# Where the four weight sums of the out projection are made: beside the second half of a streaming-encoder layer's input projection, or beside its first half

## The chip, the cores and the metric

The kernel runs on one core of one Trainium2 chip. The metric is device time in microseconds (us) of one execution; lower is better. The kernel before was run three times for its time, and one further execution was recorded by the hardware profiler; all rows of the profile below are of that one execution. In the rows, PE is the matrix engine, PEld its loading of stationary operands, DVE the vector engine, ACT the scalar engine, POOL the general engine (GpSimd), SP the engine whose instruction queue issues nearly all DMAs here.

## The reference, cut to what matters

One layer on a sequence of 2048 tokens of width 1024, in f32:

```python
u = rms_norm(h, g_mix_pre)
z = u @ w_in                      # (2048,1024) @ (1024,2816)
ya = swa_with_sinks(q, k, v of z) # sliding-window attention, 512 of the columns out
yh = hgrn2(q, f, i, g of z)       # gated linear recurrence, 512 columns out
h = h + rms_norm(concat(ya, yh) @ w_out, g_mix_post)
h = h + rms_norm(cross_attention(...), g_x_post)
h = h + rms_norm((silu(u @ w_gate) * (u @ w_up)) @ w_down, g_ffn_post)
```

What matters here are two products, the input projection `u @ w_in` and the out projection `... @ w_out`, and what the kernel prepares for the second one while the first one runs.

## The kernel before

**Every f32 operand is split in two.** A value goes into a high part rounded to the matrix engine's format and a low part (the rest), and a product is three matmuls, high by high, high by low and low by high (`products`, L1123, lines 1131 to 1133). The high part is made by ACT or POOL, the low part by DVE (`split2`, L984: lines 987, 989, 990). A product of a 512-deep half is 12 matmuls of 128x128 by 128x512.

**Large products are done by seven half-size products instead of eight** (`seven`, L1135, in the order 1, 5, 6, 3, 7, 2, 4 of `STEPS`). The stationary side comes as seven tiles S, made two products ahead (`streamed`, L1065: sums of raw quarters by DVE at line 1106, splits at 987 to 990). The moving side needs, beside the four quarters of the operand, four sums and differences of quarters. For an operand that serves many blocks these four are formed once and kept in DRAM: `sums` (L1418) makes such a DRAM tile and a generator `combined` (L1027). For the out projection that tile is `out_s`. The weight's two halves of rows are treated in turn; of each half the generator makes the sums 5, 7, 6 and 4, and each of these eight rounds has the same form: issue the DMA loads of the quarters that are new into a first row tile and a second row tile, 128x1024 f32 each; pause three times; one DVE addition or subtraction of the two row tiles in place (line 1034); one DMA store of the result to `out_s`; pause once more. The sums 5, 7 and 6 are left in the first tile and stored from there, the sum 4 in the second:

```python
            for x, y, key in (((0, 1), (0, 0), 5), ((1, 1), (0, 1), 7), (None, (0, 0), 6), (None, (1, 0), 4)):
                if x:
                    t = get(0, *x, a, b - a)
                o = get(1, *y, a, b - a)
                for _ in range(3):
                    yield
                ...
                yield
```

Where rounds 6 and 4 have no `x`, the first tile is still that of round 7. `w_out` (L1411) loads a quarter of the weight in two DMAs for the upper rows and in one for the lower ones, which makes 20 loads in all. The addition is traced inside `behind` (L1050): it is queued after the last DVE instruction that was traced when `mark` (L1058) was last called.

**The stages.** The profile's span falls into these parts around the change:

- The input projection for the first 1024 tokens (`in_first`, L451), until about 238 us. Its work comes in blocks of two groups of 128 columns (`ORDER`, L419). Columns 4 and 5, and 0 and 1, are made in four plain blocks; then come nine blocks of seven products. Counted from zero these are blocks 4 to 12 of `phases` (L1219). Blocks 5 to 8 pair a group of the recurrence's forget gate (columns 10 to 13) with a group of its query (6 to 9); the `after` part of such a block (L659) runs beside the next block and makes the gate's decays (`decays`, L726): a logarithm on ACT, two running sums on DVE, exponentials on ACT.
- The same projection for the other 1024 tokens (`in_proj`, L684), interleaved with the sliding-window attention (`swa`) and the first half of the recurrence (`hgrn`), about 262 to 623 us.
- The second half of the recurrence beside the folding of the cross-attention's weights (`fold_cross`), then the out projection and the rest of the layer as a row of jobs of `phases`.

**What sets the order.** `phases` traces a block product by product. After each product it calls `mark`, traces the stationary tiles that are needed two products on, and then lets every generator in its list `after` run to its next pause. A job's last entry, `beside`, names generators that join this list when a block begins. `in_first` gives its job an empty one, `{}` (L536). From what is traced a planner builds each engine's queue: it lists the instructions by their place in the trace and by the moment at which its own cost table has them ready. On the chip each queue then runs in order; an instruction that waits holds up all that is behind it on its engine, and the SP queue does the same for DMAs.

**Where the sums are made before.** In `mix` (L194), after nine steps of the attention and after the first half of the recurrence, `mix` creates the generator (L228), takes its first step, and lets it make four steps (one sum) behind each of the attention's last eight steps (L236). The two row tiles come from the pool `io` of that stage, under the tags `u` (two buffers) and `x` (three buffers), `io_tile` L61.

**The tiles of the first stage.** Pool `st_pool` of the first stage has the tag `pair` (five buffers of 128x2048: outputs of a block, loaded tokens, decays), `part` and `sum`. The raw quarters of the weights (`sraw`) have three buffers. The DMAs of this stage, all in the SP queue, are the weight loads, loads of the later tokens of `x` (line 663), stores of normed tokens (`un_d`) and stores of the projection (`z_d`).

Of the kernel before, what the change touches and what calls it, by code (L numbers as in the profile page):

```python
# [11 lines left out]
F32 = mybir.dt.float32  # L12
# [6 lines left out]
P = 128  # L19
T = 2048  # L20
D = 1024
# [27 lines left out]
class Layer:  # L49
# [144 lines left out]
    def mix(self):  # L194
        tc, I = self.tc, self.I
        kw = dict(reuse_waits="tile")
        with contextlib.ExitStack() as left:
            def pool(name, at, **k):
                return at.enter_context(tc.tile_pool(name=name, bufs=1, **k, **kw))

            self.mc = pool("mc", left)
            self.r_x = self.cst.tile([P, NT], F32, name="r_x")
            with (
                tc.tile_pool(name="t1", bufs=3, **kw) as self.ts,
                tc.tile_pool(name="t2", bufs=3, **kw) as self.tb,
                tc.tile_pool(name="s1", bufs=2, side="right", **kw) as self.st_pool,
                contextlib.ExitStack() as at,
            ):
                self.banks(at, "ps1", **MOST)
                self.raws = 3  # L210
                u = self.in_first()
            self.banks(left, "ps2", **FOUR)
            self.hg = pool("hg", left)
            self.wp = pool("wp", left)
            self.io = pool("io", left)
            with tc.tile_pool(name="sw", bufs=1, side="right", **kw) as self.sw:
                self.zero_tiles()
                swa = self.swa(range(NT), lambda n: "st" if n < NPB else "sth")
                hgrn = self.hgrn(range(NPB), "h")
                cols = self.in_proj(1, u)  # L220
                next(cols)
                for _ in range(NPB + 1):
                    next(swa)
                    next(hgrn)
                    next(cols)
                for _ in hgrn:
                    pass
                self.out_sums, side = self.sums("out_s", self.w_out, 4, lambda: self.io_tile("u"), lambda: self.io_tile("x"))  # L228
                side = side()
                next(side)  # L230
                pairs = self.hgrn(range(NPB, NT), "gt")
                for i, _ in enumerate(swa, NPB + 2):
                    next(cols)
                    if i == NT + 1 - 0:
                        next(pairs)
                    for _ in range(4):  # L236
                        next(side, None)
                for _ in cols:
                    pass
            phases = self.phases(self.jobs(), None, lambda: self.io_tile("z"))  # L240
            with tc.tile_pool(name="xp", bufs=1, side="right", **kw) as self.xp:
                fold = self.fold_cross()
                for _ in range(2):
                    next(fold)
                for i, _ in enumerate(pairs, 1):
                    for _ in range(2):
                        next(fold)
                    if 2 <= i < 10:
                        next(phases)
                for _ in fold:  # L250
                    pass
            left.close()
            with (
                tc.tile_pool(name="t3", bufs=3, **kw) as self.ts,
                tc.tile_pool(name="t4", bufs=3, **kw) as self.tb,
                tc.tile_pool(name="s3", bufs=2, side="right", **kw) as self.st_pool,
                contextlib.ExitStack() as at,
            ):
                self.banks(at, "ps3", **MOST)
                self.raws = 4  # L260
                for _ in phases:
                    pass
# [188 lines left out]
    def in_first(self):  # L451
# [4 lines left out]
        def x_loads(s, tiles):  # L456
            if tiles[0] == 0:
                stage.append(self.tb.tile([P, 4, D], F32, tag="T", name=f"x0_{s}", bufs=3))
            for i in tiles:
                self.load(stage[s][:, i, :], I["x"][(4 * s + i) * P:(4 * s + i + 1) * P, :])  # L460
                if s + i == 0:
                    self.g_mix = self.gain(I["g_mix_pre"])

        x_loads(0, (0, 1))
        T, raw = {}, {}
# [51 lines left out]
        def fetch():  # L517
            for s in range(2):
                for q in range(2):
# [9 lines left out]
        blocks = [("s",) + self.in_block(*p, tokens[i], tokens[i + 1], beside[i + 1], get if i > 9 else (), i < 2,  # L529
                                         None if i else lambda: x_loads(0, (2, 3)))  # L530
                  for i, p in enumerate(self.ORDER)]
# [1 line left out]
        plain = [b[1:4] + ([],) for b in blocks[:2]]  # L533
        blocks[:2] = ([(k, stream, out, lambda: iter(()), keep) for k, (stream, out, _, keep) in zip("qu", plain)]
                      + [("v", lambda kind: iter([None]), out, after, keep) for _, out, after, keep in plain])
        phases = self.phases([(lambda i, j, a, n: raw[i, j][:, a:a + n, :], 4, blocks, None, {})], T)  # L536
        PE, ACT, DVE, POOL = (getattr(mybir.EngineType, e) for e in ("PE", "Activation", "DVE", "Pool"))
        next(phases)
        self.turns("h", 36)
# [45 lines left out]
        u = []  # L585
# [1205 lines left out]
```

## Time and profile before

| what | value |
|---|---|
| time, median of 3 runs | 2554.95 us (2553.55 to 2556.43) |
| the profiled execution's own time | 2550.01 us |
| its span, first to last instruction | 2548.3 us, so 1.7 us lie around it |
| granted clock of the matrix engine, mean | 0.997 |
| matrix engine busy | 2504.8 us (98%) |
| vector engine busy | 1792.1 us (70%) |
| scalar engine busy | 1261.6 us (50%) |
| general engine busy | 364.6 us (14%) |

A busy matrix engine is not one at its peak, since its matmuls are pipelined: within a product the starts of two 128x512 matmuls are 0.227 us apart, while one is listed with 0.39 us. A product of 12 matmuls takes 2.72 us and a block of seven products 19.05 us where nothing waits. From the starts of the products in the timeline the blocks begin at 61.26 (block 4), 80.30 (5), 99.34 (6), 119.18 (7), 139.47 (8), 160.00 (9), 180.60 (10), 199.65 (11) and 218.70 us (12). A window of a block in the prediction goes by these times.

### The profile page before, as it was taken

The page shows a single profiled execution, that of the slowest core. Times are in us where ns is not written, and L with a number is a line of the kernel's source. Part 1 is how long each engine was busy: PE and PEld are TensorE (multiplying, and loading weights), DVE is VectorE, ACT ScalarE, POOL GpSimd, SP SyncE. Part 2 cuts the span into 40 slices and gives each one's busy share as a digit, 9 for nine tenths or more (in the row PEclk, how much of TensorE's full clock was granted, in tenths as well). Part 3 has the DMA queues.
Part 4 walks back from the last instruction along what each step waited for, and adds up shares of the span by engine and source line. Part 5 has one row for each costly group of instructions (what it writes and reads, how often), then busy time and mean ns, then how long its engine had stood idle before and what let it go on. Part 6 is the DMA issues. An engine that isn't in the chain of part 4 may idle for free.

```text
span 2548.3 us, 34324 instructions
## 1 busy us (share of the span) xinstructions
PE 2504.8 (98%) x12006; PEld 2092.8 (82%) x12006; DVE 1792.1 (70%) x2871; ACT 1261.6 (50%) x2635; POOL 364.6 (14%) x540
## 2 busy tenths in 40 slices
PE   9999999999999999999999999999999999999998
PEld 8878888877997778878878888888888888878886
DVE  8885488987556989988876555576566557574766
ACT  5553466655555566566753333353333335443543
POOL 4231234321311112102200000000000000000022
PEclk9999999999999999999999999999999999999999
DMA  6455655865887996867954522254465434564786
GB/s 201 146 165 178 192 154 170 230 204 146 259 292 275 316 335 189 274 206 226 333 200 146 177 91 87 74 203 148 160 210 195 144 117 159 180 188 106 228 177 151
DMA packets 387885, 486.33 MB, mean 191 GB/s; under 512 B 22272, under 2 KB 283392, under 8 KB 387712
## 3 DMA queue, kind: packets, MB, share of 16 engines
q1 hardware_dynamic: 381664, 462.12, 55.9%
q0 software_dynamic: 6048, 22.02, 5.0%
q8 instruction: 94, 1.54, 0.2%
q14 instruction: 79, 0.65, 0.1%
HBM read 317.34 MB, written 166.72 MB: 190 GB/s over the span
## 4 chain that ended last, share of the span: by engine, by line
PE 51%; DVE 2%; DMA 1%; issue 1%; ACT 1%; POOL 0%; SPq 0%; DVEq 0%; POOLq 0%; ACTq 0%
PE psm L1133 17%; PE psm L1131 17%; PE psm L1132 17%; DVE T L990 0%; DVE S L990 0%; ACT junk L1504 0%; PE pss L1390 0%; DMA out_dram<-row 0%; DMA row<-d_s 0%; DMA row<-in_w_down_dram 0%; DMA u_d<-row 0%; DMA sraw<-in_w_gate_dram 0%; DVE sum L1106 0%; ACT S L987 0%; ACT T L987 0%
## 5 line engine op out<-in xcount | busy, mean ns | idle before, releaser
L1131 PE MATMUL psm<-T,S 128*128 128x512 f32 x2680 | 1034.1, 390 | 13.3 <-ACT part L1146 7.2
L1132 PE MATMUL psm<-T,S 128*128 128x512 f32 x2680 | 1042.3, 390 | 4.0 <-DVE T L990 3.9
L1133 PE MATMUL psm<-T,S 128*128 128x512 f32 x2680 | 1029.4, 389 | 4.1 <-DVE S L990 4.1
L1131 PEld LDWEIGHTS psm<-T,S 128*128 128x128 f32 x2680 | 503.0, 188 | 125.9 <-ACT part L1146 11.9
L1132 PEld LDWEIGHTS psm<-T,S 128*128 128x128 f32 x2680 | 503.2, 188 | 110.5 <-DVE T L990 7.3
L1133 PEld LDWEIGHTS psm<-T,S 128*128 128x128 f32 x2680 | 503.1, 188 | 110.6 <-DVE S L990 6.3
L987 ACT ACTIVATE S<-sum 128x512 fp32r<-128x512 f32 (+1 forms) x370 | 224.0, 620 | 371.5 <-PE psm L1133 267.3
L990 DVE TENSOR_TENSOR S<-sraw,S 128x512 fp32r<-128x512 f32 (+1 forms) x315 | 211.5, 679 | 218.8 <-ACT S L987 215.8
L1146 ACT ACTIVATE part<-psm 128x512 f32<-128x512 f32 x285 | 168.6, 596 | 251.9 <-PE psm L1133 230.9
L990 DVE TENSOR_TENSOR S<-sum,S 128x512 fp32r<-128x512 f32 (+1 forms) x388 | 257.4, 673 | 42.1 <-ACT S L987 38.3
L987 ACT ACTIVATE S<-sraw 128x512 fp32r<-128x512 f32 (+1 forms) x300 | 184.7, 618 | 110.8 <-PE psm L1133 106.0
L1537 POOL DMA_DIRECT2D y_d<-row x16 | 14.1, 879 | 1077.9 <-DVE row L1721 1027.6
L990 DVE TENSOR_TENSOR T<-row,T 128x1024 fp32r<-128x1024 f32 (+1 forms) x112 | 131.0, 1183 | 30.2 <-ACT T L987 29.2
L157 PE MATMUL psg<-u,whi 128*128 128x512 f32 x320 | 128.3, 401 | 0.0
L158 PE MATMUL psg<-u,wlo 128*128 128x512 f32 x320 | 127.6, 399 | 0.0
L156 PE MATMUL psg<-u,whi 128*128 128x512 f32 x320 | 127.5, 399 | 0.0
L1504 ACT ACTIVATE junk<-row 128x512 f32<-128x512 f32 x160 | 99.6, 624 | 40.6 <-DVE row L1526 20.6
L987 ACT ACTIVATE T<-row 128x1024 fp32r<-128x1024 f32 (+1 forms) x112 | 113.3, 1031 | 7.5 <-DMA row<-d_s 4.3
L1672 DVE TENSOR_TENSOR row<-psm,part 128x512 f32<-128x512 f32 x66 | 43.7, 687 | 66.9 <-PE psm L1133 66.9
L1681 DVE TENSOR_TENSOR part<-psm,part 128x512 f32<-128x512 f32 x66 | 43.8, 687 | 60.1 <-PE psm L1133 59.8
L1721 DVE TENSOR_TENSOR row<-psm,part 128x512 f32<-128x512 f32 x72 | 49.1, 688 | 49.5 <-PE psm L1133 49.4
L814 ACT ACTIVATE S<-S,w_mn 128x256 f32<-128x256 f32 (+1 forms) x128 | 63.0, 496 | 29.6 <-DVE w_mn L810 29.2
(363 smaller groups left out, 3562.2 us busy)
## 6 DMA issues: line engine op xcount, KB each, us to landing
sraw<-in_w_gate_dram SPq DMA_DIRECT2D x44, 512.0 KB, 3.6
sraw<-in_w_up_dram SPq DMA_DIRECT2D x44, 512.0 KB, 3.7
hid_d<-row SPq DMA_DIRECT2D x44, 512.0 KB, 2.7
sraw<-hid_d SPq DMA_DIRECT2D x32, 512.0 KB, 4.2
sraw<-in_w_in_dram SPq DMA_DIRECT2D x44, 256.0 KB, 4.0
z_d<-pair SPq DMA_DIRECT2D x20, 512.0 KB, 3.4
raw<-in_w_in_dram SPq DMA_DIRECT2D x20, 512.0 KB, 4.8
z_d<-z SPq DMA_DIRECT2D x20, 512.0 KB, 4.0
```

The lines of the kernel that those rows point to most:

```text
L156: nc.tensor.matmul(ps, ah, bh, start=(i == 0), stop=False)
L157: nc.tensor.matmul(ps, ah, bl, start=False, stop=False)
L158: nc.tensor.matmul(ps, al, bh, start=False, stop=(i == n - 1))
L814: nc.scalar.activation(s[:, r, o:], s[:, r, o:], AF.Exp, bias=mn[:, i:i + 1], scale=-1.0, accum_out=den[:, i:i + 1])
L987: self.nc.scalar.activation(hi, raw, AF.Copy)
L990: self.nc.vector.tensor_tensor(lo, raw, f32(hi), ALU.subtract)
L1131: nc.tensor.matmul(ps, s[:, 0, k, :], t[:, 0, k, :], start=st, stop=False, **kw)
L1132: nc.tensor.matmul(ps, s[:, 0, k, :], t[:, 1, k, :], start=False, stop=False, **kw)
L1133: nc.tensor.matmul(ps, s[:, 1, k, :], t[:, 0, k, :], start=False, stop=sp, **kw)
L1146: nc.scalar.activation(t, ps, AF.Copy)
L1504: self.nc.scalar.activation(junk, a, AF.Square, scale=float(D) ** -0.5, accum_out=to)
L1721: nc.vector.tensor_tensor(d, a, b, ALU.add)
```

## The change

The creation of the sums moves from `mix` to `in_first`, and the generator becomes the `beside` of that job's block 4. It so makes one step behind each product from the start of block 4 on, 33 steps in all, instead of four behind each of eight steps of the attention. Its two row tiles are new: tags `wa` and `wb` in the first stage's `st_pool`, one buffer of 128x1024 f32 each. The loads, the eight additions and the eight stores themselves are the same.

```diff
@@ mix
-                self.out_sums, side = self.sums("out_s", self.w_out, 4, lambda: self.io_tile("u"), lambda: self.io_tile("x"))
-                side = side()
-                next(side)
                 pairs = self.hgrn(range(NPB, NT), "gt")
                 for i, _ in enumerate(swa, NPB + 2):
                     next(cols)
                     if i == NT + 1 - 0:
                         next(pairs)
-                    for _ in range(4):
-                        next(side, None)
@@ in_first
-        phases = self.phases([(lambda i, j, a, n: raw[i, j][:, a:a + n, :], 4, blocks, None, {})], T)
+        def weight_tile(tag):
+            self._n += 1
+            return self.st_pool.tile([P, D], F32, tag=tag, name=f"{tag}_{self._n}", bufs=1)
+
+        self.out_sums, side = self.sums("out_s", self.w_out, 4, lambda: weight_tile("wa"), lambda: weight_tile("wb"))
+        phases = self.phases([(lambda i, j, a, n: raw[i, j][:, a:a + n, :], 4, blocks, None, {4: [side]})], T)
```

## The prediction, on record before the result

> **What bounds the kernel now.** I read the page's first part, then the busy times of the blocks between 61 and 181 us, then who waited for whom there.
>
> ```profile
> span 2548.3 us, 34324 instructions
> PE 2504.8 (98%) x12006; PEld 2092.8 (82%) x12006; DVE 1792.1 (70%) x2871; ACT 1261.6 (50%) x2635; POOL 364.6 (14%) x540
> ```
>
> PE is the bound: it idles 2548.3 - 2504.8 = 43.5 us. An edit that leaves PE's work alone, as this one does, can only take from this idle time or add to it. So the question is where the sums stand beside a PE that waits. Next the busy times by block (columns: window, its length, then PE, PEld, DVE, ACT, POOL busy with counts, clock, DMA share, GB/s); the rows are blocks 4 to 9:
>
> ```profile
> 61.26:80.30 19.04, 19.04 (x86) 15.77 (x84) 15.78 (x20) 8.28 (x13) 3.77 (x4) 1.00 0.62 174
> 80.30:99.34 19.04, 19.04 (x86) 15.77 (x84) 11.84 (x18) 7.51 (x14) 5.02 (x8) 1.00 0.58 175
> 99.34:119.18 19.84, 19.34 (x85) 15.69 (x84) 17.58 (x25) 12.01 (x19) 7.24 (x10) 1.00 0.37 102
> 119.18:139.47 20.29, 19.34 (x85) 15.69 (x84) 19.76 (x27) 12.62 (x20) 9.90 (x11) 1.00 0.48 149
> 139.47:160.00 20.53, 19.33 (x85) 15.69 (x84) 18.63 (x25) 13.13 (x21) 9.38 (x11) 1.00 0.55 165
> 160.00:180.60 20.60, 19.65 (x87) 15.94 (x86) 19.29 (x26) 12.71 (x21) 8.18 (x10) 1.00 0.49 161
> ```
>
> Blocks 4 and 5 run at PE's pace with DVE free for 3.3 and 7.2 us. Blocks 6 to 9, beside which the decays are made, last 81.26 us, and DVE is busy 75.26 us of it (93%). They are also the ones that exceed 19.04 us. What PE waited for in blocks 4 to 9 (us, times, longest):
>
> ```profile
> PE psm L1131 <- ACT part L1146: 3.6, 4, 1.2
> ```
>
> PE waits four times, 3.6 us in all, for ACT's copy of product 5 (L1146), which frees the bank that product 3 adds to. ACT is late because this copy is queued behind the logarithm (L730), which waits for POOL's gate (L652), which waits for ACT's tanh (L650), which waits for DVE's addition (L644). Two views of that chain, ACT's timeline in block 8 and the start of block 7 on DVE:
>
> ```profile
> 140.17 1.06 ACT L429 ACTIVATE pair<-pair 128x1024 f32<-128x1024 f32 x1 [0.91 <-DMA pair<-in_x_dram]
> ...
> 145.48 1.06 ACT L730 ACTIVATE pair<-pair 128x1024 f32<-128x1024 f32 x1 [0.78 <-POOL pair L652]
> ...
> 148.35 0.59 ACT L1146 ACTIVATE part<-psm 128x512 f32<-128x512 f32 x1
> ```
> ```profile
> 120.16 1.28 DVE L644 TENSOR_TENSOR pair<-psm,part 128x512 f32<-128x512 f32 x2
> ```
> ```profile
> 121.49 0.62 ACT L650 ACTIVATE pair<-pair 128x512 f32<-128x512 f32 x1
> ```
>
> DVE's two additions end at 121.44 and ACT's tanh starts at 121.49: no slack in block 7. In block 8 ACT's chain starts with the squares of a token tile (L429) that had just arrived.
>
> **The change part by part.** Six of the eight sums (the other two, on `x`, are alike), and how DVE stood before them in all 56 such operations of the run:
>
> ```profile
> L1034 DVE TENSOR_TENSOR u<-u,x x6: 1198/1214/1224, 448.1 to 521.9; 128x1024 f32<-128x1024 f32 x6
> ...
>   DMA g<-in_w_down_dram: 7.1, 7
> ...
>   DMA qk_s<-extra: 1.1, 1
> ```
>
> *Removed from the attention's stage:* eight sums of 1.22 us, 9.8 us of DVE, between 448 and 525 us, with 20 loads and 8 stores in the SP queue. What PE waited for there:
>
> ```profile
> PE psh L805 <- DVE ys L853: 0.7, 1, 0.7
> PE pss L839 <- DVE w_mn L810: 0.5, 1, 0.5
> PE psh L849 <- DVE ptl L844: 0.3, 1, 0.3
> PE pst L839 <- DVE w_mn L810: 0.2, 1, 0.2
> ```
>
> That is 1.7 us between 425 and 550 us, all of it on DVE. The bounds of the gain are 0 and PE's whole idle time from 500 to 650 us, 5.6 us (rows at the second rival). I take **-1.7**, the waits that DVE is named for. What is late next is the attention's own chain of ACT and DVE, which the sums do not touch.
>
> *Added beside blocks 4 to 8.* One step per product; a round is four steps, so the sums come behind products 4, 8, ... 32 counted from block 4: block 4's fourth, block 5's first and fifth, block 6's second and sixth, block 7's third and seventh, block 8's fourth. The three in blocks 4 and 5, 3.7 us, fit into 10.5 us of idle DVE, where no PE wait is: nothing. Without that cover they would cost 3.7.
>
> The five in blocks 6 to 8 are 5 x 1.22 = 6.1 us for a DVE with 81.26 - 75.26 = 6.0 us left through block 9. Bounds: 0, if all idle time takes them and the lead of two products on the stationary tiles covers the rest; 6.1, if the idle time is tied to what DVE waits for. DVE's two longest waits in these four blocks:
>
> ```profile
> DVE pair L644 <- PE psm L1133: 3.6, 2, 2.4
> DVE pair L672 <- ACT pair L749: 2.2, 4, 1.3
> ```
>
> The first is for products and can take a sum; the second is for ACT's exponentials at the decays' end and leaves the chain behind it as late as before. With the two about alike I take half: **+3.1**.
>
> *The wait that the sums add.* A sum in DVE's queue needs its loads, and now there is one buffer of each tile, not two and three. Behind a waiting sum stand the low parts (L990), which PE needs, and L644, which ACT needs. The nine kinds of waits before L1034, of which the first and last are shown, add up to 29.7 us over 56 operations, 0.53 us each, most of them with single tiles. Five times that is **+2.7**. Bounds: 0, and twice that.
>
> *The loads.* They join x's token loads in one queue and on the same DMA engines:
>
> ```profile
> pair<-in_x_dram SPq DMA_DIRECT2D x8, 512.0 KB, 4.9
> ...
> row<-in_x_dram SPq DMA_DIRECT2D x16, 512.0 KB, 7.2
> ```
>
> The second row is the same load in the out projection's stage, where such sums and their loads stand beside it. If x lands 7.2 - 4.9 = 2.3 us later, block 8, where ACT already waits for it, starts its chain 2.3 us later. Bounds: 0, and 2.3 in each of blocks 7, 8 and 9, 6.9. I take **+2.3**, block 8 alone, because in the other two the lateness of DVE covers it. The eight stores follow each sum in SP; what they may hold up is the third rival. The larger pool costs nothing in time.
>
> Sum: 3.1 + 2.7 + 2.3 - 1.7 = **+6.4 us**, from the profiled execution's 2550.0 to 2556.4. The median of the runs is 4.9 us above that execution; moved by the same amount it gives **2561.4 us**.
>
> A check with another place of the trace. The out projection's sums for the next job are eight as well, made beside its blocks from 811 to 894 us in the same way:
>
> ```profile
> 811.00:894.00 83.00, 78.54 (x342) 63.44 (x341) 75.56 (x101) 46.55 (x112) 15.30 (x28) 1.00 0.94 316
> ```
> ```profile
> PE psm L1131 <- ACT S L987: 2.7, 2, 1.7
> PE psm L1133 <- DVE S L990: 1.4, 2, 1.2
> ```
>
> There DVE is 91% busy with the sums in it, and PE waits 4.1 us in these two rows. Blocks 4 to 8 would have 83.59 + 9.8 = 93.4 of 98.7 us, 95%. A loss of 4.1 less 1.7 would be +2.4, the lower part of my case's own range, +2 to +12.
>
> **The rivals.**
>
> *First, DVE takes it.* The idle 6.0 us and the lead hide all five sums. For it: DVE's waits for ACT vanish once DVE itself is late. Against it: the chain at 121.4 has no slack. It gives -1.7: 2553.3 us, up to +2.
>
> *Second, faster.* The place is the attention's tail. PE's idle time:
>
> ```profile
> 500.00:525.00 25.00, 23.83 (x124) 19.42 (x123) 21.72 (x54) 13.53 (x38) 7.39 (x9) 1.00 1.04 321
> 525.00:550.00 25.00, 24.27 (x122) 19.60 (x122) 21.80 (x62) 13.94 (x43) 8.04 (x13) 1.00 0.61 189
> 550.00:600.00 50.00, 48.99 (x267) 41.62 (x266) 41.26 (x108) 30.29 (x86) 9.68 (x21) 1.00 0.46 144
> 600.00:650.00 50.00, 47.27 (x295) 41.94 (x294) 33.53 (x58) 28.47 (x61) 6.39 (x10) 0.97 0.64 176
> ```
>
> If DVE, 87% busy from 500 to 550 us, and the DMA engines (share 1.04) pace the attention, then a tail that runs ahead keeps PE fed. The price is PE's idle time here, 1.17 + 0.73 + 1.01 + 2.73 = 5.6 us: 2549.3 us. It decides if this idle time falls under 1 us while the first stage loses less than that. Against it: in the waits above only 1.7 us carry DVE's name, and the largest part, 2.73 us, lies beyond 600 us, 75 us behind the last sum.
>
> *Third, the SP queue stands.* Three times a load must wait until the store before it has left the tile: after the first sum of each half of rows, and between the halves. Landing of those stores before:
>
> ```profile
> DMA to landing us min/median/max: 2.6/6.0/10.9
> ```
>
> Two of the three fall into block 6, and the raw weights, x and the projection's stores stand behind. If one block is held by 6.0 us on top of my sum, 2567.4 us. Against it: stationary tiles are made two products ahead, 5.4 us that cover most of such a hold.
>
> *Fourth, POOL is held by DVE.* POOL's gate, a link of the chain:
>
> ```profile
> L652 POOL TENSOR_SCALAR pair<-pair,fb,fa x8: 1196/1318/2698, 96.0 to 163.0; 128x512 f32<-128x512 f32 x8
> ```
>
> The same operation takes 1.20 to 2.70 us. If a sum stretches it by 1.22 us in each of blocks 7, 8 and 9, 3.7 us come on top: 2565.1 us; if not, nothing.
> The Trainium skill, page "SBUF — State Buffer", section "Who interferes with whom", states a rule that speaks against this change: a vector instruction with two SBUF inputs, as these sums are, and a GpSimd instruction that reads SBUF exclude each other, and the one that comes second waits for the whole of the other. By that rule the sum would be the fourth rival's, by the row's median the forecast's; the spread of the row agrees with the rule but does not show which operation held POOL.
>
> **How the numbers follow.** About 0.2%, 5.1 us, is what a measurement of this kernel can tell from no change, so same is 2549.8 to 2560.1 us. Chances: my forecast 0.50 (0.30 of it above 2560.1), the first rival 0.17 (0.16 within, 0.01 faster), the second 0.15 (0.14 faster, 0.01 within), the third 0.10, the fourth 0.08. Slower 0.30 + 0.10 + 0.08 = 0.48, same 0.20 + 0.16 + 0.01 = 0.37, faster 0.15. The range goes from 2549 (half of the second rival left out) to 2569 (the ends of the third, the fourth and of my own case left out), some 0.16 in all. The likeliest case alone: 2557 to 2567.
>
> **What would show it.** In the profile of the changed kernel blocks 6 to 9 last 85 to 90 us together instead of 81.3, with DVE over 95% busy, and PE's waits for L1146 are 8 us or more instead of 3.6; DVE sits idle before L1034 for `wa` or `wb`, 2 to 3 us; x's loads land after 7 us in block 8; PE's idle time from 425 to 550 us is 1 to 2 us smaller. Wrong would be: blocks 6 to 9 no longer than now (first rival); PE's idle time from 500 to 650 us nearly gone (second); an SP wait of 5 us for `out_s` with a late weight load behind it (third); L652 over 2.4 us in most blocks (fourth).

## The result, and the profile after

The changed kernel takes **2571.16 us** (median of 6 runs, 2568.94 to 2577.4) against 2554.25 us (6 runs, 2552.34 to 2556.43) for the kernel before on the same chip: a ratio of **1.0069, 95% interval 1.0056 to 1.0082**, 16.9 us slower. I had predicted 2561.4 us with a range of 2549 to 2569. The side was that of my likeliest chance (slower, 0.48), the size was not, and the time lies above the range. Of all the runs here and below one is left out, an execution of f1 (the kernel before with four more loads) that took 4475.97 us at a granted clock of 0.699. The profiled execution took 2569.36 us, 19.4 us more than the one of before, and the two traces are compared from here on. Lines of the input projection's front are 5 lower than before (L426 was L431, L424 was L429).

First the page's first lines.

```profile
span 2567.7 us, 34336 instructions
...
PE 2510.4 (98%) x12006; PEld 2096.4 (82%) x12006; DVE 1793.3 (70%) x2871; ACT 1260.4 (49%) x2635; POOL 363.6 (14%) x540
```

DVE has the same 2871 instructions in the same 1793 us. PE has the same 12006 matmuls, but is busy 5.6 us longer and idles 57.3 us instead of 43.5. So no engine got more work, PE waited longer, and something made the same matmuls longer.

I found where by setting the n-th product of one trace beside the n-th of the other. Block 5 starts 4.6 us later than before; block 6 loses 7.6, block 9 loses 4.4, blocks 7 and 8 together 0.3, blocks 10 and on nothing: 16.8 us up to the attention. The attention's stage takes 4.5 us less than before, the recurrence behind it 4.3 us more, and 2.7 us are added later. Some 1.7 of the 4.5 us are no work of the change: the profile of before has a stretch of half clock from 279.3 us, 3.41 us long, that this one has not.

*The opening.* SP's timeline (start, duration, queue, line, what is loaded):

```profile
18.23 1.71 SPq L75 DMA_DIRECT2D wa<-in_w_out_dram  x2
19.98 0.60 SPq L75 DMA_DIRECT2D wb<-in_w_out_dram  x1
21.14 3.67 SPq L75 DMA_DIRECT2D sraw<-in_w_in_dram  x2
24.86 0.61 SPq L75 DMA_DIRECT2D wb<-in_w_out_dram  x1
25.57 3.77 SPq L75 DMA_DIRECT2D sraw<-in_w_in_dram  x4
```

The first round's four loads, which the code issues beside block 4, stand at 18 to 25 us, 40 us ahead of it and between the raw weights. Their tiles are fresh, so nothing holds them back, and the planner brings them forward. PE's waits between 15 and 66 us, where before had none:

```profile
PE psm L1132 <- DVE u L990: 2.1, 1, 2.1
PE psm L475 <- DVE x L426: 0.4, 1, 0.4
PE psm L1131 <- POOL u L989: 0.2, 1, 0.2
```

These are 2.7 us; behind the longest one a stretch of half clock begins at 48.1 us, 3.41 us long, which costs another 1.7.

*Blocks 5 to 9.* Busy times by block (window, length, then PE, PEld, DVE, ACT, POOL, clock, DMA share, GB/s):

```profile
84.88:103.92 19.04, 19.04 (x85) 15.77 (x84) 13.24 (x19) 6.04 (x11) 3.88 (x6) 1.00 1.00 274
103.92:131.32 27.40, 21.86 (x86) 17.51 (x85) 19.93 (x27) 13.27 (x21) 9.61 (x11) 0.88 0.66 188
131.32:152.03 20.71, 19.33 (x86) 15.69 (x84) 20.02 (x26) 11.31 (x18) 8.70 (x10) 1.00 0.86 245
152.03:172.40 20.37, 19.60 (x85) 15.61 (x84) 19.47 (x26) 12.35 (x21) 9.14 (x12) 1.00 0.55 167
172.40:197.14 24.74, 21.23 (x85) 16.75 (x84) 22.68 (x30) 15.12 (x23) 9.54 (x12) 0.93 0.72 232
```

Two things are to be seen. Beside block 5 the DMA engines' busy share is 1.00, before 0.58. And blocks 6 to 9, together 93.22 us instead of 81.26, lose in two ways: PE idles 11.2 us instead of 3.6 (length less busy time, summed), and is busy 82.0 us instead of 77.7 with the same products, because the clock is 0.88 in block 6 and 0.93 in block 9. DVE is busy 82.1 of 93.2 us, 88%, less than the 93% before. PE's waits from 61 to 200 us:

```profile
PE psm L1131 <- ACT part L1146: 7.9, 4, 5.5
PE psm L1131 <- DVE pair L644: 2.8, 1, 2.8
PE psm L1131 <- ACT S L987: 0.5, 1, 0.5
```

The longest, 5.5 us, is in block 6. ACT's timeline there:

```profile
106.50 1.06 ACT L424 ACTIVATE pair<-pair 128x1024 f32<-128x1024 f32 x1 [6.00 <-DMA pair<-in_x_dram]
...
110.86 0.63 ACT L650 ACTIVATE pair<-pair 128x512 f32<-128x512 f32 x1 [1.64 <-DVE pair L644]
111.51 1.28 ACT L730 ACT_TABLE_LOAD   x1
114.28 1.06 ACT L730 ACTIVATE pair<-pair 128x1024 f32<-128x1024 f32 x1 [1.49 <-POOL pair L652]
115.35 1.28 ACT L656 ACT_TABLE_LOAD   x1
116.65 0.60 ACT L656 ACTIVATE th<-psm 128x512 f32<-128x512 f32 x1
117.14 0.59 ACT L1146 ACTIVATE part<-psm 128x512 f32<-128x512 f32 x1
```

ACT waits 6.00 us for x. In before the same squares started 1.78 us ahead of block 6 (97.56), here 2.58 us behind its start: 4.4 us later. Behind them stands the chain that the prediction described, and PE waits for its last row. Why x is late stands in SP's timeline, in the change and in before:

```profile
95.64 0.34 SPq L78 DMA_DIRECT2D out_s<-wa  x1
96.03 0.61 SPq L75 DMA_DIRECT2D wb<-in_w_out_dram  x1
...
97.33 0.61 SPq L75 DMA_DIRECT2D wb<-in_w_out_dram  x1
...
99.68 0.68 SPq L75 DMA_DIRECT2D pair<-in_x_dram  x1
```
```profile
91.96 0.60 SPq L75 DMA_DIRECT2D pair<-in_x_dram  x1
```

SP issues x 14.8 us after block 5's start, where before had 11.7: a store and two loads of the sums now stand close ahead of it. From its issue to its landing x takes 6.8 us, before 5.6. So of the 4.4 us some 3.1 are lost ahead of the issue and 1.2 in the transfer. Not all of the 3.1 need be theirs: in f1 below, with no such load there, x is issued after 13.3 us.

Block 9's wait comes from an addition itself, at DVE:

```profile
176.76 1.65 DVE L1034 TENSOR_TENSOR wb<-wb,wa 128x1024 f32<-128x1024 f32 x1 [2.06 <-DMA wb<-in_w_out_dram]
178.33 0.68 DVE L990 TENSOR_TENSOR S<-sum,S 128x512 fp32r<-128x512 f32 x1
178.93 1.21 DVE L754 SCALAR_TENSOR_TENSOR pair<-pair,pair 128x1024 f32<-128x1024 f32 x1
180.07 0.68 DVE L644 TENSOR_TENSOR pair<-psm,part 128x512 f32<-128x512 f32 x1
```
```profile
180.80 0.50 PE L1131 MATMUL psm<-T,S 128*128 128x512 f32 x1 [2.79 <-DVE pair L644]
...
182.35 0.63 PE L1132 MATMUL psm<-T,S 128*128 128x512 f32 x1
182.78 0.63 PE L1133 MATMUL psm<-T,S 128*128 128x512 f32 x1
```

DVE stands 2.06 us for a weight load and adds for 1.65; L644, three instructions behind, is what PE then waits for. After the wait PE's matmuls start 0.43 us apart, where a block at full clock has 0.23: the half clock.

### The profile page after: what moved, and what is told of

The parts are those of the page before. It is cut to its first block, busy times and chain, and to the rows that moved or that the text cites. A ratio compares the mean times of both kernels' runs of the same rounds, so it can differ in the third digit from the quotient of the medians.

```text
span 2567.7 us, 34336 instructions
## 1 busy us (share of the span) xinstructions
PE 2510.4 (98%) x12006; PEld 2096.4 (82%) x12006; DVE 1793.3 (70%) x2871; ACT 1260.4 (49%) x2635; POOL 363.6 (14%) x540
## 4 chain that ended last, share of the span: by engine, by line
PE 51%; DVE 2%; DMA 1%; ACT 1%; issue 1%; POOL 0%; SPq 0%; DVEq 0%; POOLq 0%; ACTq 0%
PE psm L1133 17%; PE psm L1131 17%; PE psm L1132 17%; DVE T L990 0%; DVE S L990 0%; PE pss L1390 0%; ACT junk L1504 0%; DMA u_d<-row 0%; DMA row<-in_w_down_dram 0%; DMA row<-d_s 0%; DVE sum L1106 0%; DMA u_s<-row 0%; ACT T L987 0%; ACT S L987 0%; DVE row L1634 0%
## 5 line engine op out<-in xcount | busy, mean ns | idle before, releaser
L1131 PEld LDWEIGHTS psm<-T,S 128*128 128x128 f32 x2680 | 503.9, 188 | 134.3 <-ACT part L1146 16.6
L990 DVE TENSOR_TENSOR S<-sraw,S 128x512 fp32r<-128x512 f32 (+1 forms) x315 | 211.8, 680 | 209.6 <-ACT S L987 207.3
L1146 ACT ACTIVATE part<-psm 128x512 f32<-128x512 f32 x285 | 168.5, 597 | 256.1 <-PE psm L1133 229.9
L990 DVE TENSOR_TENSOR S<-sum,S 128x512 fp32r<-128x512 f32 (+1 forms) x388 | 258.5, 676 | 42.9 <-ACT S L987 38.4
L990 DVE TENSOR_TENSOR T<-row,T 128x1024 fp32r<-128x1024 f32 (+1 forms) x112 | 131.1, 1183 | 27.9 <-ACT T L987 27.6
L1106 DVE TENSOR_TENSOR sum<-sraw,sraw 128x512 f32<-128x512 f32 (+1 forms) x97 | 65.7, 677 | 15.1 <-DMA sraw<-in_w_in_dram 6.6
```

What stands on the lines that cost most here:

```text
L990: self.nc.vector.tensor_tensor(lo, raw, f32(hi), ALU.subtract)
L1106: nc.vector.tensor_tensor(t, a, b, op)
L1131: nc.tensor.matmul(ps, s[:, 0, k, :], t[:, 0, k, :], start=st, stop=False, **kw)
L1146: nc.scalar.activation(t, ps, AF.Copy)
```

## The experiments

My theory after the result: four things add up, namely the early loads in the opening, the loads' bytes that make x late, the additions in DVE's order, and the half clock behind each longer wait. The rivals were that one of them explains nearly all, that the SP queue and not the DMA engines delays x, that POOL is held, and that only the place beside blocks 6 to 9 is bad.

The table has, for each kernel, its ratio to before, and from its profiled execution the us by which a section takes longer than before's: up to block 5, block 5, block 6, blocks 7 to 9, then to the attention, the attention, and the recurrence.

| kernel | ratio (95%) | to 5 | 5 | 6 | 7-9 | 10- | attention | recurrence |
|---|---|---|---|---|---|---|---|---|
| after | 1.0069 (1.0056-1.0082) | 4.6 | 0 | 7.6 | 4.7 | 0 | -4.5 | 4.3 |
| f1 first loads alone | 1.0018 (1.0006-1.0030) | 4.3 | 0 | 0.6 | 0.3 | 0 | 0.4 | 1.4 |
| e1 first loads held | 1.0061 (1.0044-1.0079) | 0.3 | 0 | 7.1 | 6.3 | 0 | -4.7 | 4.8 |
| e2 no loads | 1.0065 (1.0050-1.0080) | 3.8 | 0 | 3.0 | 6.6 | 0 | -4.1 | 2.7 |
| f4 additions alone | 1.0065 (1.0050-1.0080) | 0.6 | 4.3 | 1.4 | 7.2 | 0 | -4.5 | 5.0 |
| f3 additions twice | 1.0071 (1.0055-1.0088) | 1.0 | 0 | 4.4 | 9.4 | 0 | -5.0 | 4.8 |
| e8 no second input | 1.0049 (1.0031-1.0066) | 4.0 | 0 | 0.6 | 8.1 | 0 | -3.6 | 3.2 |
| e3 no additions | 1.0048 (1.0031-1.0065) | 1.8 | 0 | 7.3 | 1.1 | 0 | -5.1 | 3.3 |
| e6 x in other queue | 1.0056 (1.0042-1.0070) | 0 | 0 | 4.6 | 8.6 | 0 | -5.0 | 4.3 |
| e9 free block 5 | 1.0035 (1.0025-1.0044) | 0 | 0 | 5.3 | 6.7 | 0 | -3.2 | 4.7 |
| e10 quarter loads | 1.0045 (1.0030-1.0059) | 0 | 0.8 | 0.8 | 10.9 | 0 | -4.1 | 4.8 |
| e11 whole loads | 1.0061 (1.0042-1.0080) | -0.2 | 7.1 | 1.6 | 3.3 | 0 | -4.2 | 3.1 |
| e4 from block 8 | 1.0050 (1.0035-1.0065) | 0.2 | 0 | 0 | 3.6 | 4.6 | -3.0 | 3.9 |
| e5 light blocks | 1.0054 (1.0042-1.0067) | 1.0 | 0 | 0.6 | 0.3 | 0.2 | 5.6 | 5.9 |
| e7 sums nowhere | 0.9995 (0.9986-1.0004) | -0.3 | 0 | 0 | 0.2 | 0 | -4.9 | 3.0 |

A section comes from one execution; two kernels that should be alike in it differ by a few us. What is left to the end, 1 to 10 us, differs between executions mostly where the clock was halved from 820 us on, and I read nothing from it. In the attention's column 1.7 us of each gain are the half clock of before's own execution; e4, e5 and e9, whose profiles have such a stretch there too (from 287.0, 282.2 and 290.8 us), gain less or lose.

**The first loads.** f1 is the kernel before with those four loads alone:

```
+        def first_loads():
+            for tag, j in (("wa", 1), ("wb", 0)):
...
+                self.w_out(t.rearrange("p (k d) -> p k d", d=512), 0, j, 0, 2)
+            yield
...
-        phases = self.phases([(lambda i, j, a, n: raw[i, j][:, a:a + n, :], 4, blocks, None, {})], T)
+        phases = self.phases([(lambda i, j, a, n: raw[i, j][:, a:a + n, :], 4, blocks, None, {4: [first_loads]})], T)
```

> The kernel before, with only the first round's four weight loads (two for each of two tiles of their own) traced at block 4; the eight sums stay in the attention. Theory one (the opening is lost because these loads, whose tiles are free from the start, are issued ahead of the raw weights): they are issued between 15 and 25 us again, block 6 starts 4 to 5 us later than the 99.3 us of before, and blocks 6 to 9 add less than 1 us. Theory two (the opening's loss in the changed kernel is a chance of one execution, or comes from the rest of the edit): block 6 starts within 0.5 us of before. In the end time theory one gives +2 to +5 us, since part of the lead is handed back later; theory two gives no change.

SP's timeline and PE's waits from 30 to 62 us in f1:

```profile
18.23 1.73 SPq L75 DMA_DIRECT2D wa<-in_w_out_dram  x2
20.01 0.60 SPq L75 DMA_DIRECT2D wb<-in_w_out_dram  x1
21.11 3.33 SPq L75 DMA_DIRECT2D sraw<-in_w_in_dram  x2
```
```profile
PE psm L1139 <- DVE u L997: 2.0, 1, 2.0
PE psm L480 <- DVE x L431: 0.9, 1, 0.9
PE psm L1138 <- POOL u L996: 0.2, 1, 0.2
```

Theory one: the loads are at 18 us again, the opening loses 4.3 us and the whole kernel 0.18% (0.06 to 0.30), without one addition. In e1 the changed kernel has these loads queued behind the SP instruction that was traced last:

```
+            at = [self.traced(mybir.EngineType.SP)] if name == "out_s" and fresh[0] < 3 else []
+            with self.queued(*at):
+                src(t, i, j, k0, n)
```

> The changed kernel with one edit: the first round's four loads are queued in SP behind the DMA that was traced last before them, so that they stand just ahead of block 4 and no longer ahead of the raw weights at 18 to 26 us. Theory A (the SP queue: loads of the sums stand ahead of loads that the chain needs): block 4 begins at about 61.3 us again instead of 65.8, the kernel is about 4.6 us faster than the change, 2566 to 2567 us; blocks 6 and 9 stay slow. Theory B (DVE's time for the sums, 93% busy before them): no difference in blocks 6 to 9 and none to be expected in the opening, 2571.

The opening's loss is gone (0.3 us). The rest is not: blocks 6 to 9 lose 13.5 us, and the ratio's interval overlaps that of the change. So the opening is shown as a cause of 4 to 5 us there, but is not what made the change slow.

**The additions.** e2 takes the loads away; both tiles hold a constant that POOL writes once, so the output isn't the sums':

```
+            if name == "out_s":
+                if which not in fixed:
+                    fixed[which] = tiles[which]()
+                    self.nc.gpsimd.memset(fixed[which], 0.5)
+                return fixed[which].rearrange("p (k d) -> p k d", d=512)[:, :n]
```

> The changed kernel without the 20 loads of the out projection's weight: the two row tiles are filled once with a constant, and the eight additions and eight stores stay where they were (the sums are so of a constant). Theory A: the opening's 4.6 us, block 6's 7.6 us and block 9's 4.4 us go; the first half ends within 2 us of the kernel before (238.2 us), and the time is 2550 to 2556. Theory B: blocks 6 to 9 still take 5 us or more beyond the kernel before; 2560 or more.

Blocks 6 to 9 still lose 9.6 us. Its opening's 3.8 us is the edit's own: POOL's two fills stand at 1.0 and 2.3 us in front of POOL's opening work. f4 repeats it with the fills on DVE behind block 4's work:

```
-                    self.nc.gpsimd.memset(fixed[which], 0.5)
+                    with self.behind():
+                        self.nc.vector.memset(fixed[which], 0.5)
```

> The changed kernel without any load of the out projection's weights; the two tiles are filled once with a constant, by DVE behind block 4's work, and the eight additions and eight stores stay in place, so the output is not the reference's. Theory one (the additions cost by DVE's time): the opening is as before (within 0.5 us), and blocks 6 to 9 add 8 to 10 us as they did when POOL filled the tiles. Theory two (they cost only because the opening was late and its covers gone): blocks 6 to 9 add under 4 us. My prediction's term for them is 3.1 us. End time: theory one +8 to +13 us, theory two +3 us or less.

Blocks 6 to 9 lose 8.6 us, and block 5 4.3 more, which I had expected of neither theory. DVE's and PE's waits in f4:

```profile
DVE wa L1034 <- DMA out_s<-wa: 3.2, 1, 3.2
```
```profile
PE psm L1133 <- DVE S L990: 2.4, 1, 2.4
```

With no load to wait for, the second addition waits for the store before it, which still reads the one tile. DVE stands 3.2 us, the low parts (L990) behind it are late, and PE waits 2.4 us. My three additions "at nothing" in blocks 4 and 5 were at nothing only as long as DVE did not stand. f3 makes each addition twice:

```
                     nc.vector.tensor_tensor(t, t, o, op)
+                    if dst is self.out_sums:
+                        nc.vector.tensor_tensor(t, t, o, op)
```

> As the run with the additions alone, with each addition made twice (2.4 us of DVE a step instead of 1.2), so the output is not the reference's. Theory one (DVE's time in blocks 6 to 9 is the price, six additions at full price): blocks 6 to 9 add another 6 to 8 us, about 15 to 17 us in all, and block 6's start moves by less than 2 us. Theory two (what costs is each step's place in DVE's order, or its store, not its duration): blocks 6 to 9 add the same 8 to 10 us as with single additions.

Blocks 6 to 9 lose 13.8 us, 5.2 more than in f4 for six more additions of 1.21 us (7.3 us): between the two expectations, nearer to the first. Not the DVE time alone is the price, for the first six cost 8.6, the next six 5.2. Windows and PE's waits in f3:

```profile
100.35:124.62 24.27, 20.93 (x86) 16.83 (x84) 21.34 (x28) 12.07 (x19) 8.41 (x10) 0.93 0.40 126
...
166.96:195.11 28.15, 21.51 (x85) 16.80 (x84) 25.75 (x36) 14.53 (x23) 11.58 (x12) 0.88 0.60 194
```
```profile
PE psm L1133 <- ACT part L1148: 6.7, 3, 3.3
PE psm L1133 <- ACT S L987: 6.6, 2, 5.9
```

The loss sits in blocks 6 and 9, behind waits of 3.3 and 5.9 us, with the clock at 0.93 and 0.88. e8 is e2 with each addition replaced by two transposes, which read one SBUF operand:

```
+                        self.blocked(o.rearrange("p k d -> p (k d)"), t.rearrange("p k d -> p (k d)"))
```

> The third way to split the additions' cost: the kernel without loads, with each addition replaced by two 128x512 transposes of 0.64 us from one tile into the other, about as much time on DVE but with one SBUF input (out_s so holds a constant). If POOL is held by additions with two SBUF inputs: the gate on POOL takes 1.2 to 1.9 us again where it took 2.2 to 2.8, the waits before the logarithm fall from 1.9 to 3.2 us back to 0.8 to 1.5, and blocks 6 to 9 lose 3 us or less instead of 9.6. If it is DVE's time: 8 to 10 us as without loads.

Blocks 6 to 9 lose 8.7 us against 9.6 in e2. The Trainium skill (page "SBUF — State Buffer", section "Who interferes with whom"), whose rule was my fourth rival's, has a vector instruction with two SBUF inputs contend with a GpSimd instruction that reads SBUF. The links at POOL did move with the second input: ACT's waits for POOL's gate (L652) ahead of the logarithm are 10.2 us in e2, 6.3 in e8, 4.8 in before. But a loss of nearly one size with and without that input does not bear the rule out as the cause, and in the change itself these waits are 3.0 us.

**The loads.** e3 leaves the additions out and keeps loads and stores in their order, so that the stored rows are no sums:

```
-                with self.behind():
-                    nc.vector.tensor_tensor(t, t, o, op)
+                at = []
+                if dst is self.out_sums:
+                    at.append(self.traced(mybir.EngineType.SP))
+                else:
+                    with self.behind():
+                        nc.vector.tensor_tensor(t, t, o, op)
```

> The changed kernel without the eight additions on DVE: all 20 loads and eight stores stay, each queued behind the DMA traced last before it (out_s then holds quarters of the weight, not sums). Theory A: blocks 4 to 9 still lose several us to late loads of x or of raw weights, 4 to 10 us over the kernel before in the first half. Theory B: blocks 6 to 9 take what they took before, 81 us, and the time is within 2 us of the kernel before or under it.

Block 6 loses 7.3 us, blocks 7 to 9 1.1. ACT in e3 at the start of block 6, and in before:

```profile
105.32 1.06 ACT L424 ACTIVATE pair<-pair 128x1024 f32<-128x1024 f32 x1 [7.66 <-DMA pair<-in_x_dram]
```
```profile
97.56 1.06 ACT L429 ACTIVATE pair<-pair 128x1024 f32<-128x1024 f32 x1 [1.65 <-DMA pair<-in_x_dram]
```

So the loads and stores alone, with no arithmetic, make x late, and block 6 with it. Here it is all ahead of the issue: x is issued 17.6 us after block 5's start and lands 5.6 us later, as in before. Is it their place in SP's queue? e6 is e1 with x's loads issued from POOL:

```
-self.load(t[:, 0, :], self.I["x"][TB + n * P:TB + (n + 1) * P, :])
+nc.gpsimd.dma_start(t[:, 0, :], self.I["x"][TB + n * P:TB + (n + 1) * P, :])
```

> The first kernel (first round's loads held) with the five token loads of x beside the blocks issued in POOL's queue instead of SP's, so that they no longer stand behind loads and stores of the sums. If x is late because of its place in SP: its squares in block 6 begin about 17 us after the start of block 5, as in the kernel before, not 22, and block 6 loses 2 to 3 us instead of 7; 2563 to 2566. If x is late because the DMA engines are full in block 5 (busy share 0.99 there): no difference in block 6, 2568 to 2570.

x, issued at 95.25 us, has its squares at 102.46 after a wait of 6.43 us; in e1 it was issued at 96.15 and had them at 102.76. The squares came no earlier, but the run doesn't free x: in POOL's queue it stood behind a split (L989) and was issued 14.9 us after block 5's start, as late as in SP's. Block 6 lost 4.6 us, between the two expectations; its wait for L1146 is 3.6 us instead of 6.0, its half clock 3.41 us instead of 6.83. So the queue and the DMA engines are not told apart by it. e9 is e1 with `{4: [paced]}` in place of `{4: [side]}`, to empty block 5:

```
+        def paced():
+            steps = side()
+            for i in itertools.count():
+                if not 7 <= i < 14:
+                    if next(steps, steps) is steps:
+                        return
+                yield
```

> The changed kernel with the first round's loads held back as in the run of that kind, and with no step of the sums beside block 5, so that neither a load nor an addition stands there; the steps go on at block 6 and end beside block 9. Theory one (block 6 loses 7.1 to 7.6 us because the loads beside block 5 fill the DMA engines and x for block 6 lands late): the DMA share from 82 to 101 us is 0.55 to 0.65 instead of 0.98, the squares for block 6 start at most 18.5 us behind block 5's start, and block 6 loses at most 3 us, the additions' part. Theory two (block 6 loses as the first block of the decays with additions and loads beside it, wherever x is): block 6 loses 6 us or more again. Blocks 7 to 9 lose 5 to 8 us by both, as one more round stands there. The end time stays within 1.004 to 1.007 by both, since none of the blocks has room for the additions.

It did not: the next round's loads came forward into block 5, whose DMA share was 0.89, and x's squares came 1.1 us behind block 6's start. The condition failed, and the run doesn't tell the theories apart. (Its profiled execution, 2573.5 us, is also the longest of its ten; its ratio, 1.0035, is the lowest of the kernels that make whole sums there.) The pair e10 and e11 does tell them apart. Both fill the tiles once and then load at the same places, e10 a quarter of the columns, so that its rows are no full sums, e11 all 512:

```
+                self.load(d[:, :, 0:128], self.I["w_out"][r:r + p * n, j * 512:j * 512 + 128].rearrange("(k p) d -> p k d", p=p))
```

> The changed kernel with each load of the out projection's weights cut to 128 of its 512 columns: as many load instructions, at the same places, with a quarter of the bytes; the rest of both tiles is a constant written once by DVE beside block 4, so the first loads can't be issued ahead of it, and the output is not the reference's. Theory one (the loads' bytes fill the DMA engines beside block 5, and x for block 6 lands late): the DMA share of block 5 is 0.65 to 0.75, the squares for block 6 start no later than 1 us after block 6 does, and block 6 loses 1.4 to 3.5 us as without loads. Theory two (the load instructions and their waits in the SP queue hold x back): block 6 loses 6.5 us or more, as with whole loads.

> The companion of the run with a quarter of each load: the same edit with whole loads (the constant is written and then overwritten, so the output is the reference's). Both theories: block 5's DMA share 0.95 or more, the squares for block 6 start 2.5 to 4 us after block 6 does, block 6 loses 6.5 to 8 us, blocks 6 to 9 together 12 to 14 us, and the opening loses under 1 us.

Blocks 5, 6, 7 and 9, e10:

```profile
80.30:100.17 19.87, 19.37 (x85) 15.69 (x84) 12.58 (x19) 5.88 (x11) 3.86 (x6) 1.00 0.75 243
100.17:120.78 20.61, 19.35 (x86) 15.69 (x85) 20.17 (x27) 12.38 (x21) 8.92 (x11) 1.00 0.51 152
120.78:146.76 25.98, 22.24 (x85) 17.78 (x84) 21.36 (x28) 14.18 (x22) 8.71 (x11) 0.87 0.60 193
...
168.35:192.81 24.46, 20.79 (x86) 16.75 (x84) 21.53 (x29) 13.56 (x21) 8.13 (x11) 0.93 0.59 195
```

and blocks 5 and 6, e11:

```profile
80.11:106.26 26.15, 22.30 (x85) 17.67 (x84) 15.72 (x22) 6.20 (x11) 3.86 (x6) 0.87 0.91 251
106.26:127.70 21.44, 19.34 (x85) 15.69 (x84) 20.53 (x27) 11.67 (x19) 9.40 (x11) 1.00 0.60 180
```

With a quarter of the bytes in as many loads blocks 5 and 6 lose 1.6 us, with all of them 8.7: the bytes cost 7 us there, not the number of loads. They act in both ways: x is issued 14.5 us after block 5's start in e10 and 17.7 in e11, and lands 5.0 and 7.8 us later. In e10 it is issued nearly as late as in the change (14.8), and with the short transfer its squares still start 0.3 us ahead of block 6, which loses 0.8. In e11 the loss came in block 5 and not in block 6, as I had expected; there an addition at 92.39 us, late itself, stood in front of three L990, and PE waited 3.8 us for them. And e10 gained nothing by the end: its blocks 7 to 9 lose 10.9 us where e11 loses 3.3, and both are 12 us late at block 9's end. What the loads no longer take, the additions take one or two blocks later.

**Other places.** e4 is e1 with the sums begun at block 8:

```
-{4: [side]}
+{8: [side]}
```

> The generator joins at block 8 instead of block 4, with the first round's loads held as in the first kernel of this call; 33 of the 35 steps left are used, most of them in blocks 10 to 12, where DVE is idle for 4 to 9 us a block and no decays are made. Theory A: opening and block 6 as before, a loss of 0 to 4 us in block 9 where the loads still stand among the others; 2550 to 2558. Theory B: two sums fall into blocks 8 and 9, 1 to 2 us; the same range, so this one asks whether a place in the first half exists that beats both.

e5 has e9's `paced` with another condition, so that steps stand only beside block 4 and from block 10 on, where DVE is free:

```
-                if not 7 <= i < 14:
+                if i < 7 or i >= 42:
```

> The sums are made beside block 4 (seven steps) and beside blocks 10 to 12 (21 steps, the last five behind them), with no step beside blocks 5 to 9; the first round's loads are held as in the first kernel. Theory C, as the first four runs leave it (loads beside block 5 make x late for block 6, additions beside blocks 6 to 9 lengthen the chain to PE's wait, and each wait of 2 us or more is followed by a window of half clock): blocks 4 to 11 take what they took before, the first half ends within 3 us of the kernel before, and the time is 2553 to 2558. Rival D (taking the sums out of the attention is itself what costs time, wherever they go): 2562 or more with a first half that is within 3 us.

Both only moved the loss. e4 loses 3.6 us in blocks 8 and 9 and 4.6 about block 12. e5 loses 2.1 in the whole projection, and then some 7 us at the attention's start, where PE waits 5.0 us, until 283.5 us, for the first rows from `z_d`, with 10 us of half clock from 282.2 on. Its trace says what is late: DVE waits until 267.9 us for the load of the last sum, the store of that sum stands in SP at 269.1 us, and the reads of `z_d` behind it begin at 269.5 us, where before had the first of them at 258.5.

**The sums nowhere.** e7 is the kernel before without the sums' loads and additions in any place; it stores a constant instead:

```
-                self.out_sums, side = self.sums("out_s", self.w_out, 4, lambda: self.io_tile("u"), lambda: self.io_tile("x"))
-                side = side()
-                next(side)
+                self.out_sums = self.tc.dram_tile([4, P, 4 * 512], F32, name="out_s")
+                blank = self.io_tile("u")
+                self.nc.vector.memset(blank, 0.5)
+                for c in range(4):
+                    for a in range(2):
+                        self.store(self.out_sums[c, :, a * 1024:(a + 1) * 1024], blank)
```

> The kernel before without loads and additions of the out projection's sums: out_s is filled by eight stores of one constant tile at the place in the attention's stage where the sums began. It bounds what the attention's stage can gain. The recorded forecast's term (1.7 us) gives 2552 to 2553; theory D (the stage hands back whatever it gains, or loses by its new order) gives 2554 to 2560; the second rival of the forecast 2549.

The attention's stage gets 4.9 us shorter, as in nearly all the others, and PE waits once, 1.1 us, between 425 and 625 us. Yet the kernel is not faster: 0.9995 (0.9986 to 1.0004). In its profile 3.0 us are given back in the recurrence and 2.3 in the folding behind it. So, with the order that the planner then makes, the change had next to nothing to gain.

Where the recurrence gives it back, the traces show. ACT in the change, and what PE waits for most from 600 to 790 us:

```profile
647.09 1.06 ACT L987 ACTIVATE T<-z 128x1024 fp32r<-128x1024 f32 x1 [3.84 <-DMA z<-in_w_out_dram]
648.05 0.58 ACT L904 ACTIVATE vt<-pst 128x512 f32<-128x512 f32 x1
```
```profile
PE pst L925 <- ACT vt L904: 4.5, 2, 3.6
```

ACT waits for a load of `w_out` itself, and the copy that PE needs (`vt`) stands behind. SP issues the first of these loads at 633.6 us, before at 617.0: 16.6 us later, where PE's work is 11 us later, and behind the reads of the recurrence (`k`, `qq`) instead of ahead of them. All fourteen profiles without the sums in the attention have PE's wait for `vt`, 3.6 to 5.1 us; before and f1, with the sums there, have none. No run isolates it, and why the planner orders it so stays open.

## Why the prediction was wrong

*The bound and the chain were right.* PE is the bound, the loss is PE's waiting beside the decays, and L1146 behind L730, L652, L650 and L644 is where it shows: 7.9 us of waits for it, forecast as 8 or more. Blocks 6 to 9 last 93.2 us, forecast as 85 to 90.

*"They join x's token loads in one queue" is the first step that failed.* It holds for sixteen of the twenty loads. I placed them all where the code issues them; the first four went 40 us ahead of it, a term of 4.6 us in the opening that my sum lacks (f1, with these loads alone, loses 4.3 there).

*The term for x, +2.3 us, "block 8 alone", was mis-sized and misplaced.* In block 8 ACT didn't wait. x was late for block 6, whose load falls beside block 5, where I counted only DVE's idle time, and neither the loads and stores ahead of x in SP (it is issued 3.1 us later) nor the DMA engines (0.58 busy, 1.00 with the loads; the transfer takes 1.2 us longer). My 2.3 us were the transfer's alone. Block 6 lost 7.6 us; e10 and e11 give the bytes 7 us in blocks 5 and 6.

*The terms for DVE, +3.1 and +2.7, were mis-sized.* Without any load the additions cost 8.6 us in blocks 6 to 9 (f4), 9.6 in e2. My 3.1 shared DVE's idle time with the additions, as if DVE's hours were the limit. It is the delay of a chain: DVE is busy 88%, not over 95%, but an addition of 1.2 to 1.7 us in front of L644 goes down the chain to PE. The waits for the loads came to 2.1 us, close to my 2.7 in their sum, but as one wait in the worst place, not five small ones.

*What a wait sets off was missing.* I priced a wait at its length. Behind the longer ones PE ran at half clock: PE's busy time grew by 2.5 us in block 6 (21.86 for 19.34) and by 1.6 in block 9 (21.23 for 19.65).

*The gain, -1.7, was there and didn't last.* PE idles 0.7 us from 425 to 550 us, 2.0 before. The stage is 4.5 us shorter, about 3 without the half clock of before's execution. The recurrence takes it back at its start, where PE waits for `vt`; my sum took the stages behind the attention to be as before.

*The rivals.* The first (DVE takes it) is excluded by f4. The second's gain is handed back (e7). The third's mark, an SP wait of 5 us for `out_s`, came only in part: two waits for `out_s<-wa`, 5.8 us together, 3.4 the longest. No run isolates what they cost, but loads and stores of the sums ahead of others in SP are part of x's 3.1 us, and e5 shows the same at the attention's start. The fourth isn't borne out as the cause (e8), and L652's median is 1.29 us (1.32 before). My range treated these cases as exclusive; the causes found came together, and their sizes don't add up: loads alone lose 8.4 us in blocks 6 to 9 (e3), additions alone 8.6 (f4), both 13.5 (e1). Why nearly every arrangement ends between 1.0035 and 1.0071, whatever it loses up to the attention (2.1 us in e5, 16.8 in the change), stays open.

## What to carry to other kernels

Before work is moved beside another stage, take it away altogether and time that: if the kernel isn't faster without it, a new place for it has little to gain unless the order behind it changes too. Price a moved load by what stands behind it in its queue and by the DMA share of the stage into which it really comes, which for a fresh tile can be far ahead of its place in the code, and a moved operation by what stands behind it in its engine's order, not by the engine's idle share. In a stage whose chain has no slack, a wait of two or three us at the bottleneck costs its length and, more often than not, the half clock behind it.

## What the runs showed of the hardware

The half clock follows a wait of PE, but not every one. Over the 16 traces from 10 to 2500 us, counting waits of PE and whether a stretch of half clock begins in them or within 3.5 us: 1 of 123 waits of 0.9 to 1.3 us, 15 of 71 from 1.3 to 1.9, 28 of 51 from 1.9 to 2.9, and 25 of 26 above that. One wait of 1.72 us at 822 to 840 us, the same in all the traces, is followed by it in 6 of 16. The stretches last 3.41 us or two or three times that. In the 3.41 us ahead of one PE was idle for 1.6 us or more in 66 of 71 cases, about half of that time. The Trainium skill (page "TensorE: Matmul & The Clock Gate", section "🔬 Part 1: The HAM clock gate (the "warmup" mystery)") describes a window of 3413 ns that runs freely and isn't started by the kernel, and has the clock fall after an idle window; the traces agree with that length, and chance in the same wait fits a window whose edges fall anywhere. But waits well under a window's length were followed by it here.
